# Masked queries of gated linear attention: eight column scalings on ScalarE in place of two masked products on GpSimd

## The chip, the core and the metric

One core of a Trainium2 chip. The metric is the device time of one execution in microseconds (us), the median of several. The engines are TensorE (PE; its weight loads are listed as PEld), VectorE (DVE), ScalarE (ACT), GpSimd (POOL) and SyncE (SP), whose queue SPq issues nearly all DMAs. Each engine works through its own list of instructions in a fixed order and waits on semaphores for the others.

## What is computed

A decoder layer over 4096 tokens of width 1024. One input projection feeds three mixers: sliding-window attention, RWKV-7 time mixing, and gated linear attention (GLA). Each has its SiLU gate; an output projection, a norm and a residual follow. The change is in GLA, in the queries of the part inside a chunk:

```python
qc = chunks(q, GLA_KEY_DIM) * (GLA_KEY_DIM ** -0.5)
b = jnp.cumsum(g_c, axis=2)
A = jnp.einsum('bhid,bhjd,bhijd->bhij', q_c, k_c, jnp.exp(diff))   # causal
o = A @ v_c + jnp.einsum('bhid,bhdv->bhiv', q_c * jnp.exp(b), S)
```

GLA has four heads of key size 32, so the 128 key rows of all four heads fill the 128 partitions. For the products of single heads the kernel makes four copies of the scaled query, each zero outside the 32 partitions of its head.

## The kernel before

The program has two halves. The first runs over 16 strips of 256 tokens (`i` from 0 to 15) and makes the normalised input, the RWKV part and the GLA part. The second takes the strips again for attention, gates and output projection.

Work of the first half is written as generators, one per stage and strip:

- `a` normalises and transposes the input to `hT` and stores it (`hscr`); `p` holds the projections on TensorE (`pv`, `lp`, `zz`, `gqk`; fp16, 128x256 or 128x272) and makes `qg` and `kg`, the scaled GLA queries and keys, on VectorE.
- `w` makes decays and gates; `qa`, `qb`, `qc` and `q2` are the RWKV chain of a strip. `qa` makes the matrix `AT` (TensorE `atp`); `qb` writes it to memory and back (`adr`, `AS`), inverts it in 15 small VectorE steps (`TT`), and sends the result round again (`tdr`, `td`); `qc` widens the inverse by TensorE products with a VectorE copy behind each (`Xp`, `Xq`, `Xp`, `X`); `q2` walks four chunks, each `up`, a ScalarE copy `UV`, `yp`/`sp`, a VectorE state update, `rp`, and ends with a norm of `ysb` and the transposes `yt`.
- `r`, lines 1394 to 1451, is GLA. Here the masked queries `qb` are made: a tile of 128 x 4 x 128 for each of the two halves `a` of a strip (the tile has the letters of stage `qb` but nothing to do with it). They are read by the TensorE products `gap`, line 1416.
- `c` prepares weights of the second half in the gaps: it loads pieces (`cs`), splits each into a high and a low fp16 part (`ch`: the high part on ScalarE, the low one on VectorE) and stores them. Up to strip 4 these are the weights `w2` (`wscr`, 112 stores); then come the squares of the output weights, and last, in `wo_group`, their split (`woscr`, 64 stores in 16 groups). `cs` has two tiles and `ch` two, so a group cannot run far ahead of the one before.

The order is set in two steps. `emit` interleaves the generators by a model of time: the stage whose awaited tiles are ready first goes next. `Order.pin` then fixes each engine's order with a list scheduler that has its own estimates for each instruction; of what is ready it takes the lowest rank, which is the place in the emission. So an instruction that changes engine or length moves others far from it.

The second half's first tasks are mixed into the end of the first half: loads of its weights (`q0h` to `q6l`), the projections `kp`, `qp`, `vp` and the gates `gp` of strip 0, and its attention (`sc`, `pr`, `ovp`). The gates take four weights: `q3`, `q4`, `q5`, `q6`, 48 fp16 products each. Tiles of the second half lie over tiles of the first in on-chip memory, so a load can go out only when what lay there is done; `q5h` and `q5l` lie where, among others, `ch` and `cs` lay.

Of the kernel before, what the change touches and what calls it, by code (L numbers as in the profile page):

```python
# [15 lines left out]
AF = mybir.ActivationFunctionType  # L16
ALU = mybir.AluOpType
# [4 lines left out]
P = 128  # L22
# [5 lines left out]
HD = 64  # L28
# [370 lines left out]
def hybrid_kernel(ctx, tc, x, vecs, rows, ada1, adaw, w1, wl, w2, wo, w2aug, a2, gk2, cst, ctr, ctg, abias, out):  # L399
# [3 lines left out]
    S = Lane(model, nc.scalar, *LANES[1])  # L403
    G = Lane(model, nc.gpsimd, *LANES[2])
# [79 lines left out]
    def pst(tag, name, bufs=1):  # L484
        bufs = 2 if tag == "pj" else bufs
        t = ps.tile([P, 512], F32, tag=tag, name=name, bufs=bufs)
        model.take(tag, bufs, t.tensor.name)
        return t
# [7 lines left out]
    def mq(name):  # L496
        return pst("mq", name)
# [45 lines left out]
    def joint(on=True):  # L543
        model.order.joint = next(burst) if on else 0
# [72 lines left out]
    def gla_norm(osb, osq):  # L617
        S.activation(osq, osb, AF.Square)
        og = st.tile([P, 8], F32, tag="og", name="og")
        V.tensor_reduce(og, osq.rearrange("p a (h n) -> p (a h) n", n=HD), axis=AX.X, op=ALU.add)  # L620
        V.tensor_scalar(og, og, 1.0 / HD, 1e-5, op0=ALU.mult, op1=ALU.add)
        orr = st.tile([P, 8], F32, tag="orr", name="orr")
        rsqrt(orr, og, 8)
        o3 = osb.rearrange("p a (h n) -> p (a h) n", n=HD)
        V.tensor_tensor(o3, o3, orr.rearrange("p (g o) -> p g o", o=1).to_broadcast([P, 8, HD]), op=ALU.mult)

    def gla_mix(osb, dst, ot):
        for a in range(2):
            for b in range(2):
                PE.transpose(ot[:, b * NT + a * P : b * NT + (a + 1) * P], osb[:, a, b * P : (b + 1) * P], ident)  # L630
        S.activation(dst.rearrange("p b n -> p (b n)"), ot, AF.Identity, scale=vcol("gnw"))
# [14 lines left out]
    with ExitStack() as p1:  # L646
# [14 lines left out]
        def wt(shape, name, bufs=1, dt=F32, tag=None):  # L661
            tag = tag or name
            return wk1[tag].tile(shape, dt, tag=tag, name=name, bufs=bufs)
# [7 lines left out]
        def cs2(shape, name, dt=F32):  # L671
            return wt(shape, name, 2, dt, "c2")
# [33 lines left out]
        bdm = cp.tile([P, 256], F32, name="bdm")  # L706
# [687 lines left out]
        def stage_r(i):  # L1394

            e = E[i]
            yield [("p", i), ("r", i - 1)]
            qg, kg, vg, egp, egm = e["qg"], e["kg"], e["vg"], e["egp"], e["egm"]
            half = (slice(0, 64), slice(64, 128))
            qb = [cs2([P, 4, P], "qb") for _ in range(2)]  # L1400
            for a in range(2):
                G.tensor_tensor(qb[a], qg[:, a, :].rearrange("p (o n) -> p o n", o=1).to_broadcast([P, 4, P]),
                                bdm.rearrange("p (h n) -> p h n", h=4)[:, :, 0:1].to_broadcast([P, 4, P]), op=ALU.mult)
            yield [kg, "mq"]
            ktp = mq("ktp")
            for a in range(2):
                PE.transpose(ktp[:, a * P : (a + 1) * P], kg[:, a, :], ident)
            kt = wt([P, 2, P], "kt", 1)
            S.copy(kt.rearrange("p a n -> p (a n)"), ktp[:, :NT])
            for a in range(2):  # L1410
                yield [qb[a], "at", "mq"]
                gap = [pst(tag, "gap")[:, 0:NT] for tag in ("at", "mq")]
                joint()
                for hk in half:
                    for hp, sl in enumerate(half):
                        PE.matmul(gap[hp][hk], kg[sl, a, hk], qb[a][sl, 2 * hp : 2 * hp + 2, :].rearrange("p h n -> p (h n)"),
                                  start=True, stop=True)
                joint(False)

                for hp in range(2):  # L1420
                    V.tensor_tensor(qb[a][:, 2 * hp : 2 * hp + 2, :], gap[hp].rearrange("p (h n) -> p h n", h=2),
                                    gmask.rearrange("p (o n) -> p o n", o=1).to_broadcast([P, 2, P]), op=ALU.mult)
            yield [kt, "mq"]
            osb = wt([P, 2, NT], "osb", 1)
            for a in range(2):
                gidx = 2 * i + a
                Gc, Gn = Gst[gidx % 2], Gst[(gidx + 1) % 2]
                if gidx > 0:
                    V.tensor_scalar(Gc, Gc, egm[:, a, 0:1], None, op0=ALU.mult)
                kvp = mq("kvp")  # L1430
                PE.matmul(kvp[:, :NT], kt[:, a, :], vg[:, a, 0:256], start=True, stop=True)
                V.tensor_tensor(Gn, kvp[:, :NT], Gc, op=ALU.add)
                V.scalar_tensor_tensor(Gn, Gn, egp[:, a, 128:129], bdm, op0=ALU.mult, op1=ALU.mult)
                yield [Gc, qb[a], "at"]
                op_ = pst("at", "op")
                joint()
                for ht in half:
                    PE.matmul(op_[ht, :NT], qg[:, a, ht], Gc, start=True, stop=False)
                for h in range(4):
                    for ht in half:  # L1440
                        PE.matmul(op_[ht, h * 64 : h * 64 + 64], qb[a][:, h, ht], vg[:, a, h * 64 : h * 64 + 64],
                                  start=False, stop=(h == 3))
                joint(False)
                S.copy(osb[:, a, :], op_[:, :NT])
                yield [Gn, "mq"]
            osq = cs2([P, 2, NT], "osq")
            gla_norm(osb, osq)
            yield [osb, "mq"]

            gla_mix(osb, osb, mq("ot"))  # L1450
            SP.dma_start(mscr[i][:, 2 * NT : 4 * NT], osb.rearrange("p b n -> p (b n)"))
# [121 lines left out]
        for i in range(NS):  # L1573
            streams((0, "q2", stage_q2, i), (1, "k", stage_k, i), (2, "qc", stage_qc, i), (3, "qb", stage_qb, i),
                    (4, "qa", stage_qa, i), (5, "v", stage_v, i), (6, "r", stage_r, i), (7, "w", stage_d, i),
                    (8, "a", stage_a, i), (9, "c", stage_c, i), (10, "p", stage_p, i))
# [671 lines left out]
```

## Time and profile before

| | us |
|---|---|
| median of 3 runs (lowest, highest) | 2069.62 (2069.17, 2072.15) |
| the profiled execution, its own time | 2070.41 |
| span from the first to the last instruction in that profile | 2068.6 |

Nearly every instruction passes through one helper, so nearly all carry line 334; groups are told apart by their tiles. In a row of a group, `op<-gap,kg` is a result and what it was made of, `x32` the count, then busy time in us and the mean in ns of one, then the engine's idle time ahead of them and what ended it. In a row of a tile the three times are shortest, median and longest in ns, followed by the first and the last start. A row of a timeline has start and length in us, with the idle time ahead in brackets. fp32 products of TensorE appear as two records each.

### The profile page before, as it was taken

What the parts mean: (1) busy time and instruction counts of PE and PEld (TensorE: products, weight loads), DVE (VectorE), ACT (ScalarE), POOL (GpSimd) and SP (SyncE); (2) the same over time, 40 slices, a digit from 0 to 9 for tenths busy, and PEclk for the clock granted to TensorE, in tenths of its full rate; (3) what the DMA queues carried; (4) which work ended last, traced back from release to release, by engine and by line L of the source; (5) the groups of instructions that cost most, each with busy time, mean ns of one, the idle gap of its engine ahead of it and who ended that gap; (6) DMA issues with size and microseconds to landing.
All of it is one profiled execution on the core that took longest, in us unless ns stands there. A gap on an engine that the chain in (4) does not pass through costs nothing.

```text
span 2068.6 us, 61564 instructions
## 1 busy us (share of the span) xinstructions
PE 1954.1 (94%) x24931; PEld 1516.6 (73%) x24931; DVE 1610.2 (78%) x5211; ACT 1154.7 (56%) x2765; POOL 216.6 (10%) x405
## 2 busy tenths in 40 slices
PE   5899999999999999999888999999999999999997
PEld 2677777787877877777667677777877777877783
DVE  5777878878777788987767878877778877778877
ACT  5867676677766856766334444453444444444543
POOL 0510111421111111111100000000000000000000
PEclk8999999999999999999999999999999999999999
DMA  9332232334222412446314534333334333334314
GB/s 344 126 95 80 74 97 72 108 104 120 81 93 68 138 45 92 119 122 177 117 43 151 166 113 146 105 134 107 123 116 142 109 126 115 114 125 128 123 45 175
DMA packets 183898, 241.99 MB, mean 117 GB/s; under 512 B 52195, under 2 KB 141748, under 8 KB 179382
## 3 DMA queue, kind: packets, MB, share of 16 engines
q1 hardware_dynamic: 183462, 237.45, 35.5%
q8 instruction: 198, 3.24, 0.7%
q14 instruction: 94, 0.77, 0.1%
q10 hardware_dynamic: 144, 0.52, 0.1%
HBM read 177.08 MB, written 60.82 MB: 115 GB/s over the span
## 4 chain that ended last, share of the span: by engine, by line
PE 57%; DVE 24%; DMA 8%; ACT 6%; issue 3%; SPq 2%; DVEq 0%; POOL 0%; ACTq 0%; POOLq 0%
PE gp L334 16%; PE op L334 12%; PE zz L334 5%; PE qp L334 3%; PE lp L334 3%; PE sc L334 2%; SPq L334 2%; DVE mtp L334 2%; DVE q L334 2%; PE ovp L334 2%; PE kp L334 2%; DVE pr L334 2%; PE pv L334 2%; DMA cs<-in_wo 1%; DMA cs<-in_w 1%
## 5 line engine op out<-in xcount | busy, mean ns | idle before, releaser
L334 PEld LDWEIGHTS <-mtp 128*128 128x128 f16 x1344 | 130.3, 98 | 140.9 <-issue 3.5
L334 PE MATMUL op<-o,mtp 128*128 128x512 f16 x768 | 172.3, 379 | 0.1
L334 ACT ACTIVATE pr<-pr,nm,lsc 128x256 f32<-128x256 f32 (+1 forms) x256 | 149.3, 585 | 33.7 <-DVE nm L334 33.7
L334 PE MATMUL op<-ov,mtp 128*128 128x512 f16 x576 | 143.1, 379 | 0.3 <-DVE q L334 0.2
L334 PEld LDWEIGHTS <-hT 128*128 128x128 f16 x1536 | 117.1, 99 | 25.8 <-DVE kg L334 4.3
L334 DVE CUSTOM_DVE_ANT_0 pr<-sc,ab,sinks 128x256 f32<-128x256 f32 (+1 forms) x256 | 108.6, 476 | 11.4 <-PE sc L334 11.1
L334 DVE TENSOR_TENSOR yv<-op,yv 128x512 f32<-128x512 f32 x105 | 70.4, 681 | 47.8 <-PE op L334 33.7
L334 PE MATMUL pv<-gvh,hT 128*128 128x272 f16 x512 | 100.1, 286 | 6.2 <-DVE kg L334 3.1
L334 ACT ACTIVATE ag<-gp,gh 128x512 f32<-128x512 f32 x64 | 43.7, 683 | 109.4 <-PE gp L334 109.4
L334 POOL COPY kT<-kT 128x512 f16<-128x512 f16 x15 | 10.2, 677 | 845.2 <-DVE kT L334 816.0
L334 ACT ACTIVATE mtp<-yv,oi 128x1024 f16<-128x1024 f32 x30 | 34.3, 1143 | 111.7 <-DVE yv L334 111.2
L334 PE MATMUL lp<-hT,Lh 128*128 128x256 f16 x512 | 92.4, 274 | 0.1
L334 PE MATMUL zz<-hT,rh 128*128 128x256 f16 x512 | 90.4, 276 | 0.0
L334 PE MATMUL zz<-hT,vh 128*128 128x256 f16 x512 | 88.8, 273 | 1.4 <-DVE zb L334 1.4
L334 DVE SCALAR_TENSOR_TENSOR ag<-ag,gp 128x512 f32<-128x512 f32 x64 | 43.8, 684 | 59.6 <-ACT ag L334 59.5
L334 PE MATMUL zz<-hT,kh 128*128 128x256 f16 x512 | 89.8, 273 | 0.0
L334 PE MATMUL gqk<-hT,gqkh 128*128 128x256 f16 x512 | 89.4, 275 | 0.0
L334 PE MATMUL gp<-hT,q3h 128*128 128x256 f16 x512 | 86.9, 274 | 1.9 <-DVE yv L334 1.4
L334 PE MATMUL gp<-hT,q5h 128*128 128x256 f16 x512 | 87.0, 273 | 1.4 <-DVE ag L334 1.4
L334 PE MATMUL qp<-hT,q1h 128*128 128x256 f16 x512 | 85.8, 273 | 0.6 <-DVE kT L334 0.6
L334 PE MATMUL qp<-hT,q0h 128*128 128x256 f16 x512 | 85.2, 273 | 1.1 <-DVE nwt L334 1.1
L334 PE MATMUL gp<-hT,q6h 128*128 128x256 f16 x512 | 85.5, 273 | 0.0
(460 smaller groups left out, 6046.0 us busy)
## 6 DMA issues: line engine op xcount, KB each, us to landing
ov<-woscr SPq DMA_DIRECT2D x96, 512.0 KB, 3.9
xt<-in_x SPq DMA_DIRECT2D x16, 1024.0 KB, 5.3
hscr<-hT SPq DMA_DIRECT2D x16, 1024.0 KB, 5.3
hT<-hscr SPq DMA_DIRECT2D x16, 1024.0 KB, 5.1
x<-in_x SPq DMA_DIRECT2D x30, 512.0 KB, 4.3
out<-yv SPq DMA_DIRECT2D x30, 512.0 KB, 2.9
cs<-in_w SPq DMA_DIRECT2D x112, 128.0 KB, 2.4
v<-vscr SPq DMA_DIRECT2D x128, 64.0 KB, 2.5
```

The source lines that it names most:

```text
L334: r = f(*args, **kw)
```

## The change

The two GpSimd products of a strip, each of 128x512 elements with the mask `bdm` broadcast along a row, become eight ScalarE activations of 128x128, each with one column of `bdm` as its scale, one per half and head. `bdm[:, h * HD]` is 1 on the 32 partitions of head `h` and 0 elsewhere, so the values are the same.

```diff
             qb = [cs2([P, 4, P], "qb") for _ in range(2)]
             for a in range(2):
-                G.tensor_tensor(qb[a], qg[:, a, :].rearrange("p (o n) -> p o n", o=1).to_broadcast([P, 4, P]),
-                                bdm.rearrange("p (h n) -> p h n", h=4)[:, :, 0:1].to_broadcast([P, 4, P]), op=ALU.mult)
+                for h in range(4):
+                    S.activation(qb[a][:, h, :], qg[:, a, :], AF.Identity, scale=bdm[:, h * HD : h * HD + 1])
             yield [kg, "mq"]
```

Over the whole program 32 GpSimd instructions go and 128 ScalarE instructions come. Both scheduling steps see other engines and other lengths, so the order differs from the second strip on. From the second strip of attention on, TensorE's order is the same again to the end.

Three places near the end of the first half. First TensorE, in the chain of the last strip (`Xp`, `Xq`, ... are its steps; `gp` with `q6h`, `q6l` are gate products of the second half). Before:

```order
L334 MATMUL Xp<-D_18501,ATm 32x32 x32
L334 LDWEIGHTS q6h
L334 MATMUL gp<-hT,q6h 128x256
L334 LDWEIGHTS q6h
L334 MATMUL gp<-hT,q6h 128x256
L334 LDWEIGHTS q6l
L334 MATMUL gp<-hT,q6l 128x256
L334 LDWEIGHTS q6h
L334 MATMUL gp<-hT,q6h 128x256
```

Now, in two pieces, the head and the tail of the same chain:

```order
L334 MATMUL Xp<-D_18577,ATm 32x32 x32
L334 MATMUL Xq<-td,Xs 32x32 x32
L334 MATMUL Xp<-T_18665,AT 32x32 x16
L334 MATMUL X_18695<-tc_18663,Xs 32x32 x16
L334 MATMUL up<-rs,tf_544 64x64 x4
```

```order
L334 MATMUL yp<-UV,AT 64x64 x3
L334 MATMUL yt<-ident,ysb 128x128 x4
L334 MATMUL ovp<-pr,v_19055 64x128 x3
L334 LDWEIGHTS q5h
L334 MATMUL gp<-hT,q5h 128x256
```

The gate, projection and score products that stood between the steps are gone from there; from `Xp` to `yt` the chain now stands alone, and the rest of the gates (`q5`, `q6`) comes behind `yt`.

Second SyncE's queue, where the load of `q5h` stands. Before:

```order
L334 DMA adr<-AT 16x8x16 x3
L334 DMA woscr<-ch 128x2x256
L334 DMA adr<-AT 16x8x16 x5
L334 DMA q5h<-wscr 128x2048
L334 DMA q5l<-wscr 128x2048
```

Now:

```order
L334 DMA woscr<-ch 128x2x256 x2
L334 DMA o_19871<-woscr 128x2048
L334 DMA o_19872<-woscr 128x2048
L334 DMA woscr<-ch 128x2x256
L334 DMA o_19871<-woscr 128x2048
L334 DMA q5h<-wscr 128x2048
L334 DMA q5l<-wscr 128x2048
```

In both orders `q5h` follows the last `woscr` store. Before, that store stood between the `adr` stores of strip 14; now it is almost the last thing of the first half. At the last `hscr` store (the input of strip 15) 37 of the 64 `woscr` stores had been issued before, and 2 now.

Third ScalarE in the same chain (`UV` are the four copies of stage `q2`, two instructions each). Before:

```order
L334 COPY UV<-up 64x128 x6
L334 ACTIVATE ag<-gp,gh_108 128x512
L334 COPY UV<-up 64x128 x2
L334 COPY ysb<-yp 128x512
L334 ACTIVATE kT<-kp,kq_s 64x256 x4
```

Now:

```order
L334 COPY UV<-up 64x128
L334 ACTIVATE ch<-cs,wo_sc 128x2x128
L334 COPY UV<-up 64x128 x2
L334 ACTIVATE ch<-cs,wo_sc 128x2x128
L334 COPY UV<-up 64x128
L334 ACTIVATE ch<-cs,wo_sc 128x128
L334 COPY UV<-up 64x128 x2
L334 ACTIVATE ch<-cs,wo_sc 128x2x128 x2
```

Splits of the output weights now stand between the chain's copies.

## The prediction

> **What bounds the kernel now.** The first view is the busy time of each engine over the span, the second the same by stretches: columns are the stretch, its length, then busy us of PE, PEld, DVE, ACT and POOL with their instructions, TensorE's granted clock, DMA share and GB/s.
>
> ```profile
> PE 1954.1 (94%) x24931; PEld 1516.6 (73%) x24931; DVE 1610.2 (78%) x5211; ACT 1154.7 (56%) x2765; POOL 216.6 (10%) x405
> ...
> 100.00:985.00 885.00, 850.61 (x13249) 688.89 (x13243) 709.20 (x2573) 608.35 (x1426) 163.58 (x316) 0.99 0.33 100
> 985.00:1063.50 78.50, 67.49 (x991) 53.54 (x986) 56.79 (x245) 32.71 (x77) 8.40 (x13) 0.98 0.28 83
> 1063.50:1092.00 28.50, 26.21 (x507) 20.23 (x507) 19.37 (x81) 6.92 (x19) 1.57 (x4) 1.00 0.33 103
> 1092.00:1112.50 20.50, 13.45 (x200) 11.43 (x201) 10.61 (x28) 9.45 (x27) 0.61 (x1) 0.82 0.64 228
> 1112.50:2068.00 955.50, 928.72 (x9488) 698.12 (x9487) 751.73 (x2077) 429.30 (x1083) 11.41 (x15) 0.99 0.36 121
> ```
>
> TensorE is busy 94% of the span, at nearly its full clock. So the time is TensorE's work, which the change leaves alone, plus its gaps: 34.4 us in the body of the first half (885.00 less 850.61), 7.0 us from 1092.0 to 1112.5, 26.8 us in the second half. An edit elsewhere counts only where it opens or closes a gap. The second half has the same order on TensorE now as before and nothing of the change in it; I carry it at nothing. The question is the body and the seam between the halves.
>
> **The change part by part.** First the masked queries themselves: shortest, median and longest in ns, then first and last start.
>
> ```profile
> L334 POOL TENSOR_TENSOR qb<-qg,bdm x32: 1046/1048/1608, 102.0 to 995.0; 128x512 f32<-128x512 f32 x32
> ...
> L334 PE MATMUL gap<-qb,kg x256: 376/376/428, 112.7 to 1031.7; 64*64 64x256 f32 x128
> ```
>
> Their reader `gap` starts 10.7 us after them in the first strip (102.0 to 112.7) and 36.7 us after in the last (995.0 to 1031.7). Two GpSimd products take 2.1 us. Eight ScalarE ones fit into that slack even with queueing, so their own latency is off the path.
>
> Their price on ScalarE, by the group rows (busy, then mean ns) and one pair that ran back to back:
>
> ```profile
> L334 ACT ACTIVATE ch<-cs,wo_sc 128x128 f16<-128x128 f32 x16 | 6.4, 399 | 7.6 <-DMA cs<-in_wo 6.5 <-DVE D L334 1.1
> ...
> L334 ACT ACTIVATE zs<-zz,mu_s 128x256 f32<-128x256 f32 x96 | 41.7, 473 | 10.5 <-PE zz L334 9.9
> ...
> 900.66 0.82 ACT L334 ACTIVATE zs<-zz,mu_s 128x256 f32<-128x256 f32 x2
> ...
> L334 ACT ACT_TABLE_LOAD x65 | 83.4, 1283 | 1.8 <-PEq L2241 0.7
> ```
>
> The first is nearly the new operation: 128x128 with a scale per partition, 399 ns. Two `zs` of 473 take 820 together, so followers overlap by about 0.11. Eight cost 0.40 + 7 x 0.29 = 2.4 us, 16 strips 39 us. ScalarE is busy 608 of 885 us in the body, so it becomes 647, 73%, below TensorE's 96%. What reaches TensorE is only what a wait like `UV` or `zs` is pushed back by a block of 2.4 us; between 0 (all idle time) and 6 (one push of 0.4 in each strip), I take **+2**, nearer to nothing since 277 us are idle. The order has the same number of table loads, 67, before and now. The Trainium skill's page "ScalarE: Activation LUTs", in its section on table sets as the hidden batching unit, says that cheap functions, identity among them, are in every set, so none should be added; by the row above two more loads a strip would be 41 us.
>
> Second, what leaves GpSimd. It stands beside VectorE operations that take far longer than usual there:
>
> ```profile
> L334 DVE SCALAR_TENSOR_TENSOR rn<-zb,kkh,rn x32: 442/480/1265, 83.9 to 1013.1; 128x256 f32<-128x256 f32 x32
> ...
> 334.77 2.23 POOL L334 TENSOR_TENSOR qb<-qg,bdm 128x512 f32<-128x512 f32 x2 [7.15 <-DVE qg L334]
> 335.00 2.29 DVE L334 SCALAR_TENSOR_TENSOR rn<-zb,kkh,rn 128x256 f32<-128x256 f32 x2
> ...
> PE X L334 <- DVE Xs L334: 3.9, 3, 1.7
> PE pv L334 <- DVE kg L334: 3.1, 2, 1.6
> ```
>
> Two `rn` products, normally 0.48 each, take 2.29 us, and end as the pair of GpSimd products ends. Each GpSimd product can so hold VectorE by up to 1265 less 480 ns, 25 us in all 32. But VectorE isn't the bound (709 of 885), and only TensorE's waits for it can shrink. `kg`, made at the time of the masked queries, has 3.1 us; with `X` it is 7.0. I take **-3**, from 0 to -7.
>
> Third, and largest, the order at the seam. SyncE's stores (shortest, median, longest ns; first and last start) and the split's ScalarE pieces:
>
> ```profile
> L334 SPq DMA_DIRECT2D woscr<-ch x64: 326/377/1617, 796.4 to 972.9; - x64
> L334 SPq DMA_DIRECT2D hscr<-hT x16: 338/359/531, 51.7 to 899.9; - x16
> ...
> o<-woscr SPq DMA_DIRECT2D x8, 512.0 KB, 6.2
> ```
>
> The split of the output weights ran from 796.4 to 972.9, 2.80 us a store, and 37 of its 64 stores were out before the last `hscr` store at 899.9. Now 2 are. At the same pace 62 x 2.80 = 174 us remain after that point, so the last store comes at about 1074. The load of `q5h` follows it, behind loads of `o` that take 6.2 us to land, and the 48 products of gate `q5` wait for it. They, and those of `q6` with them, stand behind `yt` in the order now. What they did before is to fill the last chain. Its ends, the fillers by form from 1064.11 to 1092.02, and the pitch of one:
>
> ```profile
> 1064.11 0.74 PE L334 MATMUL Xp<-D,ATm 32*32 32x32 f32 x64 [0.62 <-DVE rd L334]
> 1092.02 0.66 PE L334 MATMUL yt<-ident,ysb 128*128 128x128 f32 x4 [1.34 <-DVE ysb L334]
> ...
> L334 PE MATMUL qp<-hT,q0h 128*128 128x256 f16 x32 | 5.3, 272 | 0.0
> L334 PE MATMUL gp<-hT,q6h 128*128 128x256 f16 x26 | 5.0, 275 | 0.0
> L334 PE MATMUL qp<-hT,q0l 128*128 128x256 f16 x16 | 4.4, 272 | 0.0
> L334 PE MATMUL gp<-hT,q6l 128*128 128x256 f16 x13 | 3.6, 274 | 0.0
> L334 PE MATMUL kp<-hT,q2h 128*128 128x256 f16 x16 | 3.0, 274 | 0.0
> L334 PE MATMUL kp<-hT,q2l 128*128 128x256 f16 x8 | 2.2, 274 | 0.0
> L334 PE MATMUL sc<-kT,q 128*128 128x256 f16 x12 | 2.1, 276 | 0.0
> ...
> 1062.67 0.38 PE L334 MATMUL gp<-hT,q6h 128*128 128x256 f16 x2
> 1062.89 0.27 PE L334 MATMUL gp<-hT,q6l 128*128 128x256 f16 x1
> ```
>
> That is 123 products. One takes 0.27 us and two 0.38, so each further one 0.11: 13.5 us of work, in a chain of 27.9 us of waits to and from VectorE and ScalarE. Now nothing stands between its steps. The chain keeps its length, and the 13.5 us come elsewhere: **+13.5**. Bounds: 0, if the fillers now lie in another gap or the chain shrinks by as much without them, and 13.5 itself, since a chain that grows is counted further down. I take the upper end, because the order leaves no filler at all between the steps.
>
> Part of it comes back right behind. Before, TensorE waited there for the softmax of strip 0:
>
> ```profile
> 1107.94 0.70 PE L334 MATMUL ovp<-pr,v 32*64 32x128 f32 x8 [5.06 <-DVE pr L334]
> 1109.93 2.41 PE L334 MATMUL ovp<-pr,v 32*64 32x128 f32 x72 [1.29 <-DVE pr L334]
> 1112.67 1.87 PE L334 MATMUL sc<-kT,q 128*128 128x256 f16 x8 [0.33 <-ACT mxa L334]
> ```
>
> In the order now, 126 gate products (13.9 us) stand between those scores and `ovp`, more than the 6.7 us of these waits: **-6**, between -6.7 and 0, the second if `q5` is late.
>
> The granted clock, third from the end of a row, moves with such gaps:
>
> ```profile
> 20.00:40.00 20.00, 13.92 (x68) 5.07 (x66) 9.27 (x37) 4.01 (x8) 0.43 (x1) 0.76 0.91 329
> ...
> 1103.00:1106.00 3.00, 0.00 (x0) 0.00 (x0) 1.83 (x8) 1.91 (x7) 0.00 (x0) 0.86 1.03 419
> 1106.00:1109.00 3.00, 0.70 (x8) 0.30 (x8) 2.94 (x6) 0.37 (x1) 0.00 (x0) 0.50 0.48 184
> 1109.00:1112.00 3.00, 2.07 (x72) 2.01 (x72) 1.57 (x2) 0.22 (x1) 0.00 (x0) 0.50 0.25 73
> 1112.00:1115.00 3.00, 2.67 (x24) 1.75 (x13) 1.82 (x6) 0.77 (x4) 0.00 (x0) 0.50 0.39 107
> ```
>
> Behind the wait for the softmax it is 0.50 for 9 us, in which TensorE is busy 5.4 us; at full clock that would be about half, so filling the wait gives back 2.7. The bare chain can lose it. Its own work is 26.2 - 13.5 = 12.7 us; at 0.76, the clock of the stretch from 20 to 40 where TensorE was busy 70%, this takes 4.0 us more, at full clock none, at 0.50 throughout 12.7. I take 4: together 4 - 2.7, or **+1**, from -2.7 to +10. The Trainium skill's page "TensorE: Matmul & The Clock Gate", in its Part 1 on the clock gate, says that the clock halves after an idle window of about 3.4 us. The 0.50 behind 5.06 us of idling agrees. As the chain's steps leave shorter gaps, by that rule the chain keeps its clock, and the sum would be 4 us lower.
>
> Two waits are added. Splits, which wait for `cs`, stand on ScalarE, VectorE and SyncE between the steps of the chain, and behind a split that waits stand `UV` and so `yp` and `sp` on TensorE.
>
> ```profile
> cs<-in_wo SPq DMA_DIRECT2D x64, 64.0 KB, 2.2
> ```
>
> A load takes 2.2 us to land, so two of them in the open would be 4.4: I take **+4**, from 0 (the loads are ahead) to 12 (more than five in the open). And gates wait for `q5h` behind the `o` loads: **+2**, from 0 (landed under the projections `qp` and `kp`) to 6.2, one landing.
>
> The sum: +2 - 3 + 13.5 - 6 + 1 + 4 + 2 = +13.5 us. The profiled execution took 2070.41, 0.8 above the median of 2069.62, so it is 2083.9 by its own time and **2083** beside the median.
>
> **The rivals.** *Covered.* The lost fillers are made up: body -3, chain +13.5 but shorter by 5 (TensorE's own products no longer stand ahead of its steps), softmax -6, no added waits: -0.5, so 2069 beside the median. For it: in before 123 fillers do delay steps by 0.1 to 0.4 each. Against it: the chain's steps wait for VectorE and ScalarE, not for fillers.
>
> *Faster.* The hold of VectorE is the larger effect: the body gains 7, the chain's loss is halved to +7, since a freer VectorE runs the splits earlier, the softmax gives -6, nothing else: -6, so 2064. For it: 25 us of VectorE time go, and the rows of `rn` show the hold plainly. Against it: VectorE has 176 idle us in the body already. The Trainium skill's page "SBUF — State Buffer", section "Who interferes with whom", has the rule for this hold: a VectorE operation with two operands in SBUF and a GpSimd one that reads SBUF exclude each other, and the second to come waits for the whole of the first. It agrees with the two rows above, and it speaks for this rival.
>
> *Worse.* The split, not the chain, sets the seam's end. At 2.80 a store it ends at 1074, and the chain at 1092; from 18 us of delay in it on, that is at a pace of 3.09 or more, `q5h` and the `o` loads come last, and TensorE stands: the splits' waits at their upper end, 12 in place of 4, and a landing of 6.2 in place of 2: +13.5 + 8 + 4.2 = +25.7, so 2095.
>
> *Not what it says.* An added table load a strip, or masked products kept: the order shows 32 GpSimd instructions gone, 128 ScalarE ones added, 67 table loads both times. I leave it out.
>
> **How the numbers follow.** About 0.2%, 4 us, is what a measurement of this kernel can tell from no change. Forecast, 2074 to 2092: 0.60. Worse, above 2092: 0.09. Covered, 2065.5 to 2073.8: 0.19. Faster: 0.12. So faster 0.12, same 0.19, slower 0.69. The range has to reach to its neighbours: below 2063 lies about half of the faster rival, 0.06, above 2098 the outer part of the worse one and what I haven't thought of, 0.06 to 0.1; together under 0.2.
>
> **What would show it.** In the changed profile: `rn` without its long ones, near 480 at most; ScalarE 39 us busier in the body and GpSimd 35 less; the last `woscr` store near 1074; TensorE idle some 13 us more between `Xp` and `yt`; no wait of 5 us ahead of `ovp`; the second half as long as before. I am wrong if the body shortens by more than 7 us, if the chain from `Xp` to `yt` comes well under 25 us, or if the last store leaves before the chain begins.

## The result, and the profile after

The changed kernel takes 2089.38 us (median of 6 runs, 2084.60 to 2092.83) against 2070.10 for the kernel before (6 runs), a ratio of 1.0089, 95% interval 1.0074 to 1.0105. It is 19 us slower; +13.5 was forecast. Its profiled execution has a span of 2086.2 us, 17.6 more than before.

The page's busy times, and the stretches of the seam (columns as in the prediction; the clock is third from the end):

```profile
PE 1962.6 (94%) x24931; PEld 1528.4 (73%) x24931; DVE 1597.1 (77%) x5211; ACT 1193.4 (57%) x2893; POOL 180.6 (9%) x373
```

```profile
100.00:985.00 885.00, 856.59 (x13568) 698.53 (x13567) 691.91 (x2581) 635.82 (x1521) 132.58 (x291) 1.00 0.31 94
...
1052.00:1064.00 12.00, 6.14 (x100) 3.99 (x100) 8.78 (x37) 3.47 (x10) 0.00 (x0) 0.66 0.39 97
1064.00:1094.50 30.50, 16.10 (x298) 13.30 (x299) 16.54 (x65) 6.32 (x17) 1.85 (x4) 0.50 0.44 124
1094.50:1103.00 8.50, 6.13 (x34) 3.97 (x33) 1.59 (x5) 2.51 (x5) 0.00 (x0) 0.50 0.92 305
...
1130.00:2086.00 956.00, 928.79 (x9514) 698.77 (x9510) 751.22 (x2078) 429.74 (x1081) 11.43 (x15) 1.00 0.37 122
```

The same 24931 TensorE records now take 1962.6 us in place of 1954.1, so 8.5 of the 17.6 us are, on balance over the span, products that ran longer. The other 9.1 are new gaps (span less busy: 114.5 before, 123.6 now). This split into busy and gaps is the way to read all runs below. The body has smaller gaps than before (28.4 us against 34.4), and the stretch behind it, from 985 to the first `Xp` of the last chain, larger ones (18.0 against 11.6); the second half has the same. The loss lies around the chain: from that `Xp` to the second strip's first `mp` it took 58.4 us before and takes 76.9 now. TensorE runs at half its clock from 1056 to 1103, and stands still for half of the last chain.

The timeline of TensorE in and around that chain (start, length, idle time ahead in brackets), and the split's stores with their first and last start:

```profile
1056.45 0.70 PE L334 MATMUL ovp<-pr,v 32*64 32x128 f32 x6 [4.67 <-DVE pr L334]
...
1062.82 1.08 PE L334 MATMUL Xp<-D,ATm 32*32 32x32 f32 x64 [0.24 <-DVE D L334]
1064.43 1.18 PE L334 MATMUL Xq<-td,Xs 32*32 32x32 f32 x64 [0.54 <-DVE Xs L334]
1066.97 1.06 PE L334 MATMUL Xp<-T,AT 32*32 32x32 f32 x32 [1.36 <-DVE T L334]
...
1085.87 0.64 PE L334 MATMUL yp<-UV,AT 128*64 128x64 f32 x6
1094.12 1.12 PE L334 MATMUL yt<-ident,ysb 128*128 128x128 f32 x4 [7.61 <-DVE ysb L334]
1097.61 1.11 PE L334 MATMUL ovp<-pr,v 32*64 32x128 f32 x6 [2.37 <-ACT ysb L334]
1098.65 0.61 PE L334 MATMUL gp<-hT,q5h 128*128 128x256 f16 x2
...
1101.06 0.42 PE L334 MATMUL gp<-hT,q6l 128*128 128x256 f16 x1
1101.27 0.64 PE L334 MATMUL gp<-hT,q6h 128*128 128x256 f16 x2
```

```profile
L334 SPq DMA_DIRECT2D woscr<-ch x64: 326/377/1468, 897.7 to 1090.6; - x64
...
L334 SPq DMA_DIRECT2D q5h<-wscr x1: 454/454/454, 1091.5 to 1091.5; - x1
```

The last 80 `ovp` of strip 0, which waited for its softmax at 1102.9 before, now wait for nothing: they stand at 1123.9, behind the gates, `kp` and part of `qp`. But the first `ovp` of the strip, which stood inside the full chain before (at 1068.5), now stand ahead of it and wait there, from 1051.8. What filled that place before were the products of gate `q5`, whose weights were loaded by then; now `q5h` comes late here too. First before, then now:

```profile
L334 PE MATMUL gp<-hT,q5h x512: 272/273/283, 1054.4 to 2011.4; 128*128 128x256 f16 x171
L334 SPq DMA_DIRECT2D q5h<-wscr x1: 382/382/382, 975.8 to 975.8; - x1
```

```profile
L334 PE MATMUL gp<-hT,q5h x512: 272/273/421, 1098.7 to 2028.6; 128*128 128x256 f16 x171
```

Behind this wait the clock is 0.50, and the chain with its holes doesn't bring it back: `yt` takes 1.12 us in place of 0.66, and the gate products behind it follow each other at 0.21 us in place of 0.11. The 7.61 us ahead of `yt` are VectorE's norm of `ysb` (1.21 us of them a wait of VectorE for a weight split that stands in the middle of the norm); before, 48 `qp` products lay there. The last store of the split goes out at 1090.6, and `q5h` right behind it.

The masked queries themselves are as costed: eight in a row take 2.45 us where 2.4 was worked out.

```profile
330.77 2.45 ACT L334 ACTIVATE qb<-qg,bdm 128x128 f32<-128x128 f32 x8
```

### The profile page after: what moved, and what is told of

Read it like the earlier page. It is cut to its first block, busy times and chain, and to the rows that moved or that the text cites. A ratio compares the mean times of both kernels' runs of the same rounds, so it can differ in the third digit from the quotient of the medians.

```text
span 2086.2 us, 61636 instructions
## 1 busy us (share of the span) xinstructions
PE 1962.6 (94%) x24931; PEld 1528.4 (73%) x24931; DVE 1597.1 (77%) x5211; ACT 1193.4 (57%) x2893; POOL 180.6 (9%) x373
## 4 chain that ended last, share of the span: by engine, by line
PE 64%; DVE 19%; DMA 7%; ACT 6%; issue 2%; SPq 2%; DVEq 0%; POOL 0%; ACTq 0%; POOLq 0%
PE gp L334 16%; PE op L334 12%; PE zz L334 7%; PE qp L334 4%; PE lp L334 3%; PE pv L334 2%; PE gqk L334 2%; SPq L334 2%; PE sc L334 2%; DVE mtp L334 2%; PE ovp L334 2%; PE kp L334 2%; DVE q L334 2%; DVE pr L334 2%; DMA woscr<-ch 2%
```

## Experiments

Two theories stood at first. **Order**: the engine of the masked queries matters little; the changed kernel loses because the rearranged seam leaves the last chain empty. **Engine**: 39 us more on ScalarE hold up the chains themselves. Each run shared a chip with runs of the kernel before, and ratios are to those.

### The new engine in the old order, and the reverse

In both kernels the steps that set the order are told the other engine than the one that does the work. The instructions put in are placed by the model's start times.

```diff
-                G.tensor_tensor(qb[a], ...)
+                def put(*_, **__):
+                    made = [nc.scalar.activation(qb[a][:, h, :], qg[:, a, :], AF.Identity, scale=bdm[:, h * HD : h * HD + 1])
+                            for h in range(4)]
+                    model.order.other = ("Activation", [m.ins for m in made])
+                    return made[-1]
+                G.put = put
+                G.tensor_tensor(qb[a], ...)
```

> The eight ScalarE scalings in place of the GpSimd products, but both steps that set the order still count the work as two GpSimd products; so TensorE, VectorE and SyncE keep the order of before row for row, and ScalarE has the new instructions put in where the products would have started. Theory order (the loss comes only from the rearranged seam): 2064 to 2071 us, ratio 0.997 to 1.000, the last woscr store near 973 and the last chain from Xp to yt 28 us with its fillers. Theory engine (39 us more on ScalarE hold up the chains themselves): 2080 us or more in spite of the old order. The gap of TensorE from 100 to 985 us tells what VectorE gains when GpSimd no longer holds it: 28 us as in the changed kernel if the freed VectorE is the cause, 34 us as before if it was the order.

Measured: 2069.48 us, ratio 0.999 (0.9974 to 1.0005). Theory order. The stretch of the body and of the last chain, and the masked queries (line 1420 is where the instructions of `put` are issued):

```profile
100.00:985.00 885.00, 851.12 (x13312) 690.01 (x13303) 700.07 (x2590) 644.24 (x1549) 130.61 (x286) 1.00 0.34 101
1063.00:1092.00 29.00, 26.78 (x416) 20.66 (x404) 17.55 (x71) 9.14 (x23) 1.58 (x4) 1.00 0.38 129
```

```profile
L1420 ACT ACTIVATE qb<-qg,bdm x128: 384/386/402, 102.6 to 992.6; 128x128 f32<-128x128 f32 x128
```

ScalarE has 36 us more in the body, VectorE 9 less, and TensorE's gaps are 33.9 us where they were 34.4. So the two terms of the change itself come to nothing together. Each by itself is not nothing. Of TensorE's waits in these 885 us, by the engine that ended them, those for VectorE fell from 28.4 to 18.3 us, those for ScalarE rose from 3.0 to 10.9, and the rest rose from 2.5 to 4.4. Rows of before, then of e1 (who waits, what ended it, us in total, times, longest; in e1 the helper's line is 351):

```profile
PE X L334 <- DVE Xs L334: 3.9, 3, 1.7
...
PE yp L334 <- ACT UV L334: 0.8, 1, 0.8
...
PE ktp L334 <- ACT UV L334: 0.5, 1, 0.5
```

```profile
PE sp L351 <- ACT UV L351: 3.3, 5, 1.3
PE X L351 <- DVE Xs L351: 2.7, 3, 1.6
...
PE wssp L351 <- ACT UV L351: 2.1, 1, 2.1
```

Three of the waits for ScalarE, 3.4 us together (at 333, 691 and 934 us), stand right behind a block of the new activations on ScalarE; `kg` and `X` together fell from 7.0 to 4.2. So by this trace ScalarE's work does push the chains, and VectorE's freed time does shorten gaps, by about as much. A wait is put down to what came last, so part of the shift may be one wait that changed its name; how much each would be without the other is not shown.

> The reverse: the two GpSimd products are issued, but the order is set as if the eight ScalarE scalings were there; the rows differ from those of the changed kernel by a few exchanges in the last two strips only, and the last chain has no filler. Theory order: 2085 to 2097 us, ratio 1.008 to 1.013, the last woscr store near 1090 and the granted clock at 0.50 through the last chain. Theory engine: 2066 to 2075 us, since ScalarE is no busier than before.

Measured: 2095.78 us, ratio 1.0104 (1.0083 to 1.0125). GpSimd does the work as before, and the kernel is as slow as the changed one. Its body has gaps of 31.8 us, 22.2 of them waits for VectorE and 7.7 for ScalarE; in the changed kernel it is 28.4, with 19.1 and 8.3. With the new order held too, then, the change itself takes some 3 us out of the body, from one profile each (a second profile of the changed kernel, e5, has 29.9), which is less than the times of these two kernels can tell apart.

```profile
L351 SPq DMA_DIRECT2D woscr<-ch x64: 326/377/1144, 909.2 to 1102.5; - x64
```

```profile
1075.50:1106.00 30.50, 16.76 (x366) 13.53 (x365) 17.71 (x71) 6.59 (x18) 1.86 (x4) 0.56 0.41 119
```

The split ends late, and in the last chain (here from 1075.6 to 1106.0) TensorE is busy 16.8 of 30.5 us at a clock of 0.56, without any new instruction on ScalarE. The engine theory, that the 39 us on ScalarE make the loss, falls with these two runs.

### Which step of the ordering does it

> The eight ScalarE scalings, counted as ScalarE instructions in the last step that fixes the order, but in the emission, which interleaves the stages, still as two GpSimd products. 38 of 64 woscr stores come before the last hscr store, and 141 products of the second half stand in the last chain. Theory emission (the split slips because the emission hands stage c its turns later): 2062 to 2072 us, ratio 0.996 to 1.001. Rival (the list scheduler's places for the scalings cost by themselves): over 2076 us.

Here the emission's clocks see two GpSimd products, and the list scheduler sees the eight ScalarE instructions. Measured: 2064.88 us, ratio 0.9972 (0.9958 to 0.9987), a little faster than before, with the last `woscr` store at 965.2. So the slip comes from the emission: with the new instruction in its model of ScalarE it hands stage `c` its turns later. By which of its rules was not traced further.

### The weight split moved ahead

```diff
-                    (8, "a", stage_a, i), (9, "c", stage_c, i), (10, "p", stage_p, i))
+                    (8, "a", stage_a, i), (7.5, "c", stage_c, i), (10, "p", stage_p, i))
```

> The changed kernel with one number changed: in the emission the weight-preparing stage c ranks ahead of stage a in place of behind it (7.5 for 9), so all 64 woscr stores are issued before the last hscr store, and 128 products of the second half stand in the last chain. Theory order: the loss goes, 2062 to 2071 us, ratio 0.996 to 1.001, clock 1.00 in the last chain. Theory engine: still 2080 us or more. A third way: the splits, now in the middle of the body, push other work on VectorE and ScalarE and cost there what the seam gains, 2075 to 2085 us.

Measured: 2069.52 us, ratio 0.9979 (0.9966 to 0.9993): one rank gives the whole loss back.

```profile
1063.00:1092.00 29.00, 27.09 (x457) 20.79 (x455) 18.56 (x77) 7.55 (x21) 1.58 (x4) 1.00 0.35 120
```

The chain is full again, at a clock of 1.00. The body pays some of it, as the third way had it: its gaps are 40.4 us.

> The kernel before with the same number changed (7.5 for 9): 42 in place of 37 of the 64 woscr stores come before the last hscr store, and the last chain has 140 products of the second half in place of 135. Theory order: next to nothing to gain, 2064 to 2072 us, ratio 0.997 to 1.001. If an earlier split is worth something by itself, also with the seam filled, it is below 2062 us, and then the gain of the changed kernel with an earlier split can't be put down to the seam alone.

Measured: 2076.26 us, ratio 1.0013 (1.0000 to 1.0027). In the kernel before, whose seam was filled already, the same number gains nothing, and the body's gaps grow to 40.2 us. The time came out above the range of both expectations; that nothing is gained where the seam is full agrees with the theory of the order.

> The changed kernel with stage c still further ahead in the emission (5.5 for 9, ahead of the attention part r too); all woscr stores leave before the last hscr store, as with 7.5, and the last chain is as full. If the gain of an earlier split is the seam alone, it is the same as with 7.5: 2064 to 2071 us, ratio 0.996 to 1.000. If splitting earlier costs the body something (with 7.5 TensorE's gaps from 100 to 985 were 40.4 us against 28.4 in the changed kernel and 34.4 before), they grow further, to 43 us or more, and the time to 2070 to 2078 us.

Measured: 2063.90 us, ratio 0.9964 (0.9948 to 0.9979), the lowest ratio of all, though not told apart from the 0.9972 above. The gaps of the body did not grow further, they are 36.2 us: the second theory, that an earlier split costs the body more, failed.

> The kernel before with stage c ahead of r in the emission (5.5 for 9): GpSimd products, all woscr stores before the last hscr store, 138 products of the second half in the last chain. Beside the changed kernel with the same number (ratio 0.9964) it tells what the engine is worth in a good order. If the engine matters little either way, within 3 us of that: ratio 0.995 to 0.998. If it is VectorE freed of GpSimd that made that kernel fast, this one is slower by 3 us or more: 2066 us or more, ratio 0.998 or more.

Measured: 2081.01 us, ratio 1.0052 (1.0036 to 1.0068).

> The ScalarE scalings with the emission's old clocks and the earlier split together; 140 products of the second half in the last chain. The two changes mend the same place, so they don't add: 2060 to 2068 us, ratio 0.995 to 0.999, against 0.9972 and 0.9964 for each alone. If they add, it is below 0.994.

Measured: 2077.56 us, ratio 1.0034 (1.0021 to 1.0046).

Both have a full last chain and are yet slower than before. e11 is a miss on either side; e10 falls, by its numbers, on the side of the freed VectorE: it takes 17 us more than the changed kernel with the same rank. The busy time says where most of it went. First e10's, then e11's page, then two stretches of the body in e10 and the same two before:

```profile
PE 1967.2 (94%) x24931; PEld 1524.4 (73%) x24931; DVE 1610.7 (77%) x5211; ACT 1154.5 (55%) x2765; POOL 211.5 (10%) x405
```

```profile
PE 1964.1 (95%) x24931; PEld 1521.0 (73%) x24931; DVE 1596.5 (77%) x5211; ACT 1190.9 (57%) x2893; POOL 174.7 (8%) x373
```

```profile
460.00:470.00 10.00, 7.96 (x85) 6.30 (x85) 6.70 (x15) 5.87 (x18) 1.42 (x3) 0.74 0.75 273
...
720.00:730.00 10.00, 8.87 (x98) 6.64 (x101) 9.01 (x22) 3.18 (x9) 0.00 (x0) 0.83 0.27 74
```

```profile
460.00:470.00 10.00, 10.00 (x175) 8.61 (x173) 9.35 (x28) 6.94 (x18) 0.00 (x0) 1.00 0.09 26
720.00:730.00 10.00, 10.00 (x184) 7.53 (x180) 6.20 (x25) 8.00 (x24) 0.50 (x3) 1.00 0.53 173
```

The same products take 13.1 and 10.0 us longer than before. Gaps of some 2.5 to 3.5 us in the body (2.59 and 3.39 close together, ahead of 457.3 and 462.0, and 2.96 ahead of 721.1) go with a stretch at a lower clock (0.74 and 0.83 of 10 us, so some 2 us each). In these two orders there are more of them: between 100 and 985 the clock is at half for 10 us in before, for 31 in e10 and for 34 in e11; an estimate from this, with half of that time lost, is 10 to 12 us, near the 13.1 and 10.0. So the order also sets how often TensorE falls to half its clock in the body.

The rest of e10's loss is gaps, 42.6 us in the body against 36.2 in e8 (29.6 of them waits for VectorE against 21.0). That agrees with a VectorE held by GpSimd, but the two orders differ, so it isn't isolated; and e11, with VectorE freed, is slow as well, so freeing it isn't enough. Of the engines by themselves the pairs with the order held speak: before with e1, and e2 with the changed kernel.

### What the half clock costs

The last question is how the 17.6 us divide between work that no longer fills the chain and the low clock. Products whose results nobody reads are put into the waits of the last chain of the changed kernel. They save nothing, so the lost fillers stay lost. This is the last form (e12), with one of the places:

```diff
+            z, w = [t[:, 0:P].bitcast(F16).rearrange("p (n two) -> p n two", two=2)[:, :, 1] for t in (by, ident)]
+            for _ in range(n):
+                PE.matmul(keep["t"][:, 0:P], w, z, start=True, stop=True)
...
+                warm(i, Sc.rearrange("p b n -> p (b n)"), 7)
                 rs = wt([P, 2, HD], "rs", 2)
```

The changed kernel once more, on the chip of the first of these runs:

> The changed kernel once more, unaltered, on the chip of the next three, so that they can be set against it: 2084 to 2093 us, ratio 1.007 to 1.011.

Measured: 2091.21 us, ratio 1.0091 (1.0076 to 1.0107).

> The changed kernel with products added that compute nothing used: behind each step of the last chain (Xp, Xq, X, and in each chunk rp, up, yp) 6 to 15 fp32 products of 128x128, and 60 between the last yp and yt, each depending on the step before, so that they fall into its waits; no product of the second half stands in the chain, as in the changed kernel. They save no work, so the lost fillers stay lost. Theory clock (besides the lost fillers, half the clock from about 1054 to 1103 us costs the chain and the gates behind it): the granted clock is back at 1.00 in the chain, which takes 28 to 30 us for 31, and the time falls to 2079 to 2085 us, ratio 1.004 to 1.007. Theory fillers only (the chain waits for VectorE and ScalarE, the clock is of no account): the same as the changed kernel or longer by the added products, 2087 us or more.

Measured: 2106.95 us, ratio 1.0165 (1.0141 to 1.0189). Mis-sized: the 60 products ahead of `yt` took 13.5 us for a wait of 7.6, and the chain took 46.9 us. The score products had also gone behind the chain. It says nothing on the question.

> Like the run with idle products, with smaller ones and fewer (fp32, 64 columns instead of 128; 3 behind each step of a chunk, 4 behind Xp, Xq and X, 54 between the last yp and yt) and in another bank of PSUM, so that the attention products ahead of the chain stay where the changed kernel has them; one look at how long one takes decides whether they fit the waits. They save no work. Theory clock: the granted clock is near 1.00 for most of the chain, which takes 27 to 30 us from Xp to yt in place of 31, the gates behind yt run at full clock, and the time is 2079 to 2087 us, ratio 1.004 to 1.008. Theory fillers only: 2088 us or more, ratio 1.009 or more.

Measured: 2113.15 us, ratio 1.0210 (1.0196 to 1.0224). A miss of another kind: the clock did not come back in the whole chain (58 products stand ahead of `yt`, where 54 were announced).

```profile
1064.00:1094.00 30.00, 28.31 (x281) 25.31 (x282) 8.97 (x27) 4.64 (x13) 0.00 (x0) 0.50 0.30 86
1094.00:1121.00 27.00, 26.64 (x139) 26.10 (x138) 5.51 (x32) 1.11 (x3) 0.00 (x0) 0.50 0.07 28
```

> The changed kernel with idle products of the kind that the lost fillers were: fp16, here 128x128, each from the step before (7 behind each step of a chunk, some 10 behind Xp, Xq and X, 88 between the last yp and yt), about 0.06 us each at full clock, so some 13 us in the whole chain. They save no work, and no product of the second half stands in the chain. Theory clock: the granted clock comes back to 1.00 within the first third of the chain, which takes 28 to 30 us from Xp to yt in place of 31; the gates behind yt run at full clock; 2079 to 2087 us, ratio 1.004 to 1.008. Theory fillers only: 2088 us or more, ratio 1.009 or more. If the clock stays at 0.50 for long, as with the small fp32 products, the run says nothing on its price.

Measured: 2081.02 us, ratio 1.0058 (1.0035 to 1.0081), about 7 us below the changed kernel, though it does 207 products more (100 of them ahead of `yt`, where 88 were announced). The two intervals overlap a little, so the 7 us are uncertain by nearly as much; six of its eight runs lie at 2078 to 2082 us and two at 2088.

```profile
1064.00:1076.00 12.00, 9.10 (x143) 7.43 (x140) 5.22 (x16) 3.48 (x9) 0.00 (x0) 0.72 0.22 61
1076.00:1090.50 14.50, 12.56 (x232) 11.18 (x232) 8.90 (x44) 2.64 (x7) 0.00 (x0) 1.00 0.53 174
1090.50:1103.00 12.50, 12.50 (x132) 11.00 (x133) 4.15 (x16) 5.88 (x16) 0.00 (x0) 1.00 0.78 261
```

The clock is back from about 1076. The chain is no shorter by it (32.6 us from `Xp` to `yt`, 31.3 in the changed kernel; part of it still at half clock and with the idle products in it). The gain lies behind `yt`: from there to the scores of the second strip, from which the orders agree, it takes 30.8 us in place of 37.1. Of these 6.3 us, 2.4 are the wait of `ovp` for `ysb` (2.37 above), which is covered here because 30 gate products happen to stand ahead of that `ovp`; the remaining 3.9 are products at full clock. From the chain's first `Xp` to the second strip's `mp` it is then 71.9 us, against 76.9 in the changed kernel and 77.1 in its second profile (e5). So the run with idle products is faster by some 5 us in this stretch; that the clock has some 4 of the 6.3 and the exchange 2.4 is read from the traces, not isolated. Within the chain itself the clock is not shown to cost anything.

### All profiled executions side by side

| run | ratio | span | TensorE busy | gaps | last `woscr` |
|---|---|---|---|---|---|
| before | 1 | 2068.6 | 1954.1 | 114.5 | 972.9 |
| changed | 1.0089 | 2086.2 | 1962.6 | 123.6 | 1090.6 |
| ScalarE, old order (e1) | 0.9990 | 2067.2 | 1951.5 | 115.7 | 969.1 |
| GpSimd, new order (e2) | 1.0104 | 2100.0 | 1968.9 | 131.1 | 1102.5 |
| changed, emission's old clocks (e7) | 0.9972 | 2060.3 | 1952.1 | 108.2 | 965.2 |
| changed, split at 7.5 (e3) | 0.9979 | 2068.4 | 1954.8 | 113.6 | 913.6 |
| changed, split at 5.5 (e8) | 0.9964 | 2064.0 | 1956.4 | 107.6 | 829.9 |
| before, split at 5.5 (e10) | 1.0052 | 2084.9 | 1967.2 | 117.7 | 835.1 |
| before, split at 7.5 (e4) | 1.0013 | 2078.7 | 1959.2 | 119.5 | 980.2 |
| old clocks and split at 5.5 (e11) | 1.0034 | 2075.6 | 1964.1 | 111.5 | 825.6 |
| changed, once more (e5) | 1.0091 | 2090.9 | 1963.8 | 127.1 | 1094.0 |
| changed, idle fp32 products (e6) | 1.0165 | 2108.7 | 1993.8 | 114.9 | 1088.3 |
| changed, smaller idle fp32 products (e9) | 1.0210 | 2108.8 | 2003.4 | 105.4 | 1084.2 |
| changed, idle fp16 products (e12) | 1.0058 | 2076.1 | 1965.5 | 110.6 | 1081.7 |

In the last three rows the idle products count as busy.

## Why the prediction was right, and where its sum was not

The sign, the place and the main cause held: the change by itself comes to about nothing, and the seam's order makes the loss. That the sum came within 6 us of the measured time is partly luck, since several terms were off in opposite directions. The terms, one by one:

- **ScalarE, +2.** In the old order TensorE's waits for ScalarE rose by 7.9 us (e1), 3.4 of them right behind the new blocks; in the new order by 0.6 (e2 against the changed kernel). The mechanism, a push of what waits behind a block, is there; its size depends on the order.
- **VectorE freed, -3.** TensorE's waits for VectorE fell by 10.1 us in the old order (e1) and by 3.1 in the new one; VectorE's own busy time fell by 14.2 (1610.2 to 1596.0 over the span). In the old order the two terms cancel: gaps of 33.9 us against 34.4. The hold was real: 10 of the 32 `rn` products took over 600 ns before, 4 in e1 and 2 in the changed kernel, where GpSimd has other work left. Of the 6.0 us by which the body's gaps shrank in the changed kernel, some 3 come with its order, since e2 with GpSimd has 31.8.
- **Lost fillers, +13.5.** TensorE's gaps from `Xp` to `yt` grew from 1.7 us to 14.5, with the last of them: +12.8. The largest term was the right one, and nearly of the right size.
- **Softmax wait, -6.** Between `yt` and the second strip's first product of that kind (`mp`) the gaps fell from 7.2 to 3.3, so -3.9; the wait of the last `ovp` went, as forecast. But the strip's first `ovp` now wait for the softmax ahead of the chain, 4.67 us from 1051.8, and the gaps from 985 to the chain grew by 6.4. The prediction worked out the late `q5` for the chain alone and has no term for this place. The body's -6.0 hides it in the sum.
- **Clock, +1.** This step failed, in size: over the whole span the products take 8.5 us longer. (Not all of that is time lost: inside the chain a longer product may only fill a wait.) The prediction supposed that the bare chain would lower the clock, and took 0.76 for it. The clock fell before the chain began, at the end of the softmax wait ahead of it; the chain, busy for 16 of 30 us, did not raise it again, and so it stayed at 0.50 from about 1056 to 1103, over the chain and 9 us of work behind it. Filled idly (e12), the kernel is some 5 to 7 us faster. The rule of the Trainium skill weighed there ("TensorE: Matmul & The Clock Gate", Part 1) was used on a premise that did not hold: the bare chain does leave a longer gap than its window, the 7.61 us ahead of `yt`. And in these traces shorter gaps lower the clock too: in the changed kernel it falls behind 2.44 us without a product (1033.2 to 1035.6), to 0.72 over the stretch from 1034 to 1040:

```profile
1034.00:1040.00 6.00, 4.38 (x26) 3.53 (x26) 5.91 (x33) 2.55 (x6) 0.00 (x0) 0.72 0.39 111
```

- **Splits between the chain's steps, +4.** The chain is 3.4 us longer (31.3 against 27.9), but this holds the low clock too. The timeline separates them in part: in two of the chunks a split stands between the copies `UV`, and from `up` to `up` these take 4.88 and 4.48 us, where the next one without it takes 3.95; and one split holds the norm ahead of `yt` by 1.21 us. So the step of the prediction is seen at work; its whole price was not isolated.
- **Wait for `q5h`, +2.** None: the gates start 0.0 us behind the `ovp` ahead of them. The split ended later than worked out (1090.6 for 1074, at 3.06 us a store for 2.80), yet the load had landed by 1098.65.

The rival *faster*, by the freed VectorE, is refuted as a forecast of the time; its mechanism exists, but in the old order (e1) the waits for ScalarE grow by about what it gains. *Covered* fell with the 12.8 us of gaps. *Worse* was nearer than its chance of 0.09 said: its price of a late split did not come due, but the clock brought the time to 2089, between the forecast and its 2095.

## What to carry to other kernels

Where a scheduler sets the order, the price of moving an operation is the price of the order that comes out; the operation was worth 0.999 here, with two effects of opposite sign in it, and its side effect 1.010. A sum of nothing is not yet two terms of nothing: look at who ended the waits. Such a change is measured fairly with the old order held, and the order can then be mended by a rank. In a kernel bound by TensorE, read busy and gaps apart at an equal count of products: a gap costs itself and then, by the clock, the work behind it until the clock is back (here 47 us at 0.50).

## What was not expected of the hardware

TensorE can look busy and stay at half its clock. With small fp32 products (64 columns, a weight load ahead of each) it was busy 28.3 of 30 us and then 26.6 of 27, and the granted clock was 0.50 for all of the 57 us (e9). With fp32 products of 128 columns in the same places, and more of them (e6), it was 1.00 over a stretch as busy:

```profile
1070.00:1100.00 30.00, 29.64 (x467) 27.06 (x465) 9.85 (x30) 5.58 (x16) 1.57 (x4) 1.00 0.36 110
```

With fp16 products (e12) it came back in a stretch that was busy only 9.1 of 12 us. So the recorded busy time isn't what the gate goes by. The Trainium skill's page "TensorE: Matmul & The Clock Gate", Part 1, says that some 3.4 us of sustained activity bring the clock back; by its rule e9 should have had it within its first microseconds if busy records were activity. The runs show that they are not; how many columns in a microsecond are enough wasn't tried.
